# An encoder trunk in fp32: the begin of the MLPs in another order, and the joint to the down projection

## The chip, the cores and the metric

The kernel runs on one core of a Trainium2 chip. The metric is the device time of one execution in microseconds (us), lower is better. The core's engines each take their own list of instructions in order and wait for one another by semaphores: PE multiplies matrices, DVE and ACT work on whole tiles, POOL does tile sums and issues some transfers, SP issues most transfers. TensorE's clock has two levels here, 1.2 and 2.4 GHz; the profile gives the granted clock as a share of the full one.

## The reference

Two requests of 256 and 512 tokens, 768 in all, with 1024 features pass through two layers. Layer 0 has two kinds of attention, layer 1 a differential attention, and each has an MLP behind it:

```
def rmsnorm(x, g, eps=NORM_EPS):
    xf = x.astype(jnp.float32)
    y = xf * lax.rsqrt(jnp.mean(xf * xf, axis=-1, keepdims=True) + eps)
    return (y * g.astype(jnp.float32)).astype(x.dtype)
...
# every layer, after attention: x = x + relu(rmsnorm(x, g) @ w_up) ** 2 @ w_down
```

The hidden width of the MLP is 4096. Everything is fp32.

## The kernel before, in words

**Precision.** Each fp32 operand is halved into a high part (a copy by ACT, L80 for weights, L116 and L119 for activations) and a low part (a subtraction by DVE, L81, L117, L120), and a product is three passes on PE: high by high, high by low, low by high.

**Tokens and features.** Features lie on the partitions, tokens along the rows. The 768 tokens are two halves A and B of 384 (`HT`).

**Up projection** (`product`, L857). It makes the 4096 hidden features in 16 blocks of 256, `mp` 0 to 15. A product is 12 matmuls: four slices of 128, three passes each. The blocks 0 and 1 are made in the plain way, 8 products each, since their operands `c0` to `c3` are the norm-scaled x alone. The blocks 2 to 15 take a scheme with seven products instead of eight: its operands are sums of the four quarters of x (`c4` to `c7`, made once by `second()`, L792 and L117, and kept) and sums of the four quarters of the weights (`weights()`, four sums on POOL, L843, then the halving of four pieces for the products (1,4), (6,5), (7,3) and (2)). The seven results are joined on DVE and ACT into a tile `z` (L865, L926, L939), in which four quarters of 384 tokens lie.

**The norm.** x is multiplied by the norm's gain before the projection, but by the tokens' factor 1/rms only after it. The squares of x are made by ACT and added up on DVE (`acc`, L152), summed over the partitions on PE (`ss`, L161, 12 tiny matmuls), turned into a mean on DVE (`ms`, L164), raised to -1/2 on POOL (`rt`, L166), and spread over all partitions on PE (`pb`, L178) with a copy by DVE (`R`, L180).

**Finishing a block** (`finish`). z is cut at zero and multiplied by R on DVE (L876), squared by ACT (L878), and sent to a buffer `T` in DRAM by ACT's queue (L879); four further quarters `t`, sums of those, are made on DVE (L865, L792) and sent by POOL's queue (L887). For the blocks before R is there, z waits in the list `wait`. Three z tiles exist.

**Down projection** (L1019). It takes the same scheme the other way round: 7 products, each over the whole hidden width in `NG` groups of `ND` = 4 blocks, 28 steps of 48 matmuls. A step's right operand `th` is loaded from T (`operand`, a transfer by SP) and halved by ACT (L116) and DVE (L117); its weights are loaded, summed on POOL (L985) where needed, and halved. The first four steps use four banks of PSUM at once, one each for 256 output features.

**Order.** The program is written in one order for all engines; a scheduler then sets each engine's list by a model of when each instruction could run, so an edit in one place can move instructions elsewhere in the lists. Tiles come from pools with a fixed number of buffers.

## Time and profile before

| | |
|---|---|
| median of 3 runs | 1789.31 us (1788.85 to 1790.62) |
| profiled execution | 1793.21 us |
| its span | 1791.2 us |
| granted clock of TensorE, mean | 0.982 |
| PE busy | 96% of the span |
| DVE busy | 77% |
| ACT busy | 46% |
| POOL busy | 33% |

The profile is of one execution. A row of its timeline begins with the start in us from the span's begin and the busy time in us; then come engine, line of the kernel, operation, the names of what is written and read, and in brackets the idle time before and what ended it. Rows that follow each other closely are put together (x2, x3). A row's time contains its start-up, so consecutive ones overlap a little. PE's matmuls are pipelined, and a few records are missing.

### The profile page before, as it was taken

The numbers are of one execution on the slowest core, as the hardware profiler recorded it, in microseconds if no ns is written. First come the engines' busy times: TensorE is split into PE (matmuls) and PEld (weight loads), VectorE is DVE, ScalarE is ACT, GpSimd is POOL, SyncE is SP. The second block draws the span as 40 slices with busy tenths as digits, with TensorE's granted clock in tenths as the row PEclk, the third lists the DMA queues.
The fourth block names the chain that finished last, engine by engine and source line by source line (L and its number), as shares of the span: only waits on it lengthen the run. The fifth ranks groups of instructions, "written<-read, shape, count | busy, mean of one in ns | idle before, by whom it ended". The sixth has DMA issues, their size and how long they took to land.

```text
span 1791.2 us, 28400 instructions
## 1 busy us (share of the span) xinstructions
PE 1728.0 (96%) x10994; PEld 1644.2 (92%) x10994; DVE 1385.5 (77%) x2182; ACT 827.2 (46%) x1509; POOL 583.7 (33%) x456
## 2 busy tenths in 40 slices
PE   7999999998999999999999999999988999999997
PEld 7887888898999989999999999988988999899997
DVE  7777746597888867799656767776878888787995
ACT  6665544363333444444435555554633334444441
POOL 2321000023555404475021212220225554053750
PEclk8999999999999999999999999999999999999998
DMA  5111223312554587664311101112125545977621
GB/s 173 41 33 37 68 71 104 121 48 72 189 163 164 182 329 294 245 204 158 97 46 48 48 25 45 54 57 95 48 69 180 166 166 170 337 271 258 223 89 71
DMA packets 74598, 235.42 MB, mean 131 GB/s; under 512 B 7904, under 2 KB 25056, under 8 KB 74464
## 3 DMA queue, kind: packets, MB, share of 16 engines
q1 hardware_dynamic: 52480, 186.93, 31.1%
q0 software_dynamic: 7168, 25.17, 3.8%
q10 hardware_dynamic: 14816, 21.52, 3.3%
q8 instruction: 86, 1.41, 0.3%
q14 instruction: 48, 0.39, 0.1%
HBM read 182.47 MB, written 50.33 MB: 130 GB/s over the span
## 4 chain that ended last, share of the span: by engine, by line
PE 79%; DVE 10%; issue 4%; ACT 3%; POOL 2%; DMA 2%; POOLq 0%; DVEq 0%; SPq 0%; ACTq 0%
PE dn L1019 26%; PE up L857 18%; PE dqk L190 8%; PE opa L202 5%; PE dvp L190 4%; PE opb L202 2%; PE npa L202 2%; PE ds L268 2%; PE dpv L716 2%; DVE t L792 2%; DVE wlo L81 1%; PE qp L190 1%; PE vp L190 1%; PE npv L596 1%; PE npb L202 1%
## 5 line engine op out<-in xcount | busy, mean ns | idle before, releaser
L857 PE MATMUL up<-c,whi 128*128 128x384 f32 x1824 | 472.8, 341 | 3.0 <-DVE z L865 3.0
L1019 PE MATMUL dn<-th,whi 128*128 128x384 f32 x1792 | 464.6, 340 | 8.4 <-DVE th L117 5.7
L857 PEld LDWEIGHTS up<-c,whi 128*128 128x128 f32 x1824 | 335.6, 191 | 3.7 <-issue 3.6
L1019 PEld LDWEIGHTS dn<-th,whi 128*128 128x128 f32 x1792 | 328.4, 189 | 9.7 <-DVE th L117 6.3
L857 PE MATMUL up<-c,wlo 128*128 128x384 f32 x912 | 311.0, 342 | 13.3 <-DVE wlo L81 13.1
L1019 PE MATMUL dn<-th,wlo 128*128 128x384 f32 x896 | 304.4, 340 | 0.0
L985 POOL TENSOR_TENSOR ch<-ch,wd 128x1024 f32<-128x1024 f32 x60 | 190.7, 3189 | 127.6 <-DVE wlo L81 97.4
L843 POOL TENSOR_TENSOR s<-wraw 128x512 f32<-128x512 f32 x56 | 91.7, 1652 | 368.8 <-DMA wraw<-in_w_up_dram 284.9
L81 DVE TENSOR_TENSOR wlo<-ch,whi 128x1024 fp32r<-128x1024 f32 x88 | 165.7, 1894 | 36.6 <-ACT whi L80 35.1
L857 PEld LDWEIGHTS up<-c,wlo 128*128 128x128 f32 x912 | 173.9, 191 | 15.4 <-DVE wlo L81 15.4
L80 ACT ACTIVATE whi<-ch 128x1024 fp32r<-128x1024 f32 x88 | 93.4, 1064 | 184.7 <-PE dn L1019 147.1
L1019 PEld LDWEIGHTS dn<-th,wlo 128*128 128x128 f32 x896 | 169.7, 189 | 0.0
L81 DVE TENSOR_TENSOR wlo<-wraw,whi 128x1024 fp32r<-128x1024 f32 (+3 forms) x132 | 146.7, 1114 | 27.5 <-ACT whi L80 27.1
L80 ACT ACTIVATE whi<-wraw 128x1024 fp32r<-128x1024 f32 (+3 forms) x128 | 117.0, 916 | 91.6 <-PE up L857 42.7
L117 DVE TENSOR_TENSOR th<-tr,th 128x1536 fp32r<-128x1536 f32 x56 | 131.3, 2347 | 7.6 <-ACT th L116 7.0
L190 PE MATMUL dqk<-whi,xh 128*128 128x256 f32 x384 | 115.9, 302 | 3.1 <-ACT dv L646 3.1
L190 PE MATMUL dqk<-whi,xl 128*128 128x256 f32 x384 | 108.5, 283 | 0.0
L190 PE MATMUL dqk<-wlo,xh 128*128 128x256 f32 x384 | 108.3, 282 | 0.0
L701 ACT ACTIVATE de<-ds,m 128x512 f32<-128x512 f32 (+1 forms) x96 | 58.3, 612 | 81.7 <-DVE m L699 81.7
L878 ACT ACTIVATE z<-z 128x1536 f32<-128x1536 f32 x32 | 47.7, 1490 | 103.0 <-DVE z L876 103.0
L865 DVE TENSOR_TENSOR z<-up,z 128x384 f32<-128x384 f32 x168 | 92.4, 551 | 2.6 <-issue 1.3
L80 ACT ACTIVATE whi<-s 128x1024 fp32r<-128x1024 f32 x56 | 59.5, 1064 | 67.0 <-PE up L857 67.0
(217 smaller groups left out, 3784.4 us busy)
## 6 DMA issues: line engine op xcount, KB each, us to landing
wd<-in_w_down_dram SPq DMA_DIRECT2D x84, 512.0 KB, 4.1
tr<-T SPq DMA_DIRECT2D x56, 768.0 KB, 5.4
wraw<-in_w_up_dram SPq DMA_DIRECT2D x64, 512.0 KB, 3.6
T<-t POOLq DMA_DIRECT2D x64, 384.0 KB, 3.1
T<-z ACTq DMA_DIRECT2D x32, 576.0 KB, 3.0
ch<-in_w_down_dram SPq DMA_DIRECT2D x28, 512.0 KB, 6.0
wraw<-in_w_in_o_dram SPq DMA_DIRECT2D x24, 512.0 KB, 3.6
wraw<-in_w_in_e_dram SPq DMA_DIRECT2D x16, 512.0 KB, 3.6
```

Of the source, the lines that this page charges most:

```text
L80: nc.scalar.activation(hi, raw, AF.Copy)
L81: nc.vector.tensor_tensor(out=lo, in0=raw, in1=hi.bitcast(F32), op=ALU.subtract)
L117: nc.vector.tensor_tensor(out=lo, in0=src, in1=hi.bitcast(F32), op=ALU.subtract)
L190: nc.tensor.matmul(ps[:, :256], st[:, tk], col(k, part, 0, 256), start=(k == 0 and i == 0), stop=(k == KD - 1 and i == 2))
L202: nc.tensor.matmul(ps[:, : e - s], w, mv[:, s:e], start=(k == 0 and i == 0), stop=(k == nk - 1 and i == 2))
L701: nc.scalar.activation(e, s, AF.Exp, bias=m, scale=1.0, accum_out=l2[:, c : c + 1])
L843: nc.gpsimd.tensor_tensor(out=d_, in0=x_, in1=y_, op=ALU.add)
L857: nc.tensor.matmul(ps, part[a_][:, base + k * P : base + (k + 1) * P], t[:, b_], start=start and k + i == 0, stop=stop and k == 3 and i == 2)
L865: nc.vector.tensor_tensor(out=out, in0=x_, in1=y_, op=op)
L878: nc.scalar.activation(z, z, AF.Square)
L985: nc.gpsimd.tensor_tensor(out=t, in0=t, in1=new.pop((i, rp)), op=ALU.add)
L1019: nc.tensor.matmul(ps, w[a_][:, c : c + P], th[:, b_, q], start=i + q + k == 0, stop=i == NG - 1 and q == ND - 1 and k == 2)
```

## The change

The changes lie in `mlp` (both layers), and in the norm behind layer 0's MLP.

- `weights()`: the four sums on POOL are written ahead of all splits; the splits come in the order (1,4), (7,3), (2), (6,5) instead of (1,4), (6,5), (7,3), (2).
- `finish()`: of the two tiles for sums, the first is taken from another pool in even blocks.
- The norm's squares are written ahead of the plain products; the column sums and `rt` after the first half of the second plain block; the spreading to R right behind the plain blocks, ahead of block 2. Before, squares and column sums stood behind block 2, the spreading behind the first product of block 3.
- The weights of block 2 are written ahead of `second()`.
- The waiting z of blocks 0 and 1 are finished inside block 2, and block 2's own z at its end; before, all three at the begin of block 3.
- In each block the sum with p3 stands ahead of the product p5.
- Down projection, step 0: for all four banks the passes with the high half of `th` come first, then those with the low half.
- Norm behind layer 0's MLP: squares in two tiles in turn.

```
-            for ps_, t in (((1, 4), raws[0]), ((6, 5), sa), ((7, 3), sb), ((2,), raws[1])):
-                if t is sa:
-                    for d_, x_, y_ in ((s1, a21, a22), (s2, s1, a11), (s3, a11, a21), (s4, a12, s2)):
-                        nc.gpsimd.tensor_tensor(out=d_, in0=x_, in1=y_, op=ALU.add)
+            for d_, x_, y_ in ((s1, a21, a22), (s2, s1, a11), (s3, a11, a21), (s4, a12, s2)):
+                nc.gpsimd.tensor_tensor(out=d_, in0=x_, in1=y_, op=ALU.add)
+            for ps_, t in (((1, 4), raws[0]), ((7, 3), sb), ((2,), raws[1]), ((6, 5), sa)):
...
+            if mp == FF // 256 - 1:
+                ta, tb = (up.tile([P, 1024], F32, tag="s", name="t", bufs=3)[:, :NT].rearrange("p (a t) -> p a t", a=2) for _ in range(2))
+            else:
+                ta, tb = (xo_tile("t").rearrange("p (a t) -> p a t", a=2) if mp % 2 == 0 and n == 0 else
+                          g1.tile([P, 2, HT], F32, tag="c0", name="t", bufs=4) for n in range(2))
...
         ws = [weights(True) for _ in range(2)]
+        for k in MO:
+            nm.add(x[k])
         for w in ws:
...
+                if last == 0 and wait:
+                    rt = nm.rstd()
...
             if len(wait) == 1:
+                w2 = weights()
                 second()
+        R.append(nm.spread(rt))
...
-            w = weights()
+            w = weights() if mp > 2 else w2
             one = lambda n: product(bank(n), w[n], n)
             p1 = one(1)
-            if mp == 3:
-                R.append(nm.spread(rt))
-                while wait:
-                    finish(wait.pop(0))
...
             add(z11, p2, z11)
+            if mp == 2:
+                finish(wait.pop(0))
             p4 = one(4)
             add(z22, one(7), z12)
             add(z21, p4, z22, ALU.subtract)
+            add(z12, p3, z12)
+            if mp == 2:
+                finish(wait.pop(0))
             p5 = one(5)
             nc.vector.scalar_tensor_tensor(out=z22, in0=p5, scalar=-1.0, in1=z22, op0=ALU.mult, op1=ALU.subtract)
             add(z12, p5, z12)
-            add(z12, p3, z12)
-            if mp == 2:
-                for k in range(KD):
-                    nm.add(x[k])
-                rt = nm.rstd()
-                wait.append(z)
-            else:
-                finish(z)
+            finish(z)
...
+            for passes in (((0, 0), (1, 0)), ((0, 1),)) if s == 0 else (((0, 0), (0, 1), (1, 0)),):
+                for r, ps in enumerate(banks):
+                    w = parts[n, i, r // 2]
+                    for q in range(ND):
+                        c = (r % 2) * 512 + q * P
+                        for a_, b_ in passes:
+                            nc.tensor.matmul(ps, w[a_][:, c : c + P], th[:, b_, q], start=i + q + a_ + b_ == 0,
+                                             stop=i == NG - 1 and q == ND - 1 and a_ == 1)
...
-        nxt, nn = [None] * KD, Norm(sq)
+        nxt, nn = [None] * KD, Norm(sq2)
```

**PE, begin of layer 0's MLP.** The rows are matmuls in PE's order; `up_` is a product's bank (4951 is the last product of block 2, 5026 the first of block 3, 5082 the second), `c` an operand. Before:

```order
L857 MATMUL up_4951<-c5_4733,whi_4855 128x384 x2
L857 MATMUL up_4951<-c5_4733,wlo_4856 128x384
L161 MATMUL ss_4989<-ones_77,acc_4327 128x2 x6
L857 MATMUL up_5026<-c1_4374,whi_5006 128x384 x2
...
L857 MATMUL up_5026<-c1_4512,wlo_5007 128x384
L178 MATMUL pb_5040<-ident_72,rt_4998 128x128 x4
L178 MATMUL pb_5046<-ident_72,rt_4998 128x128 x2
L857 MATMUL up_5082<-c3_4380,whi_5018 128x384 x2
```

Now (up_4788 and up_4785 belong to the second plain block, up_4911 is the first product of block 2):

```order
L856 MATMUL up_4788<-c3_4518,wlo_4552 128x384
L161 MATMUL ss_4837<-ones_77,acc_4327 128x2 x6
L856 MATMUL up_4785<-c2_4377,whi_4555 128x384 x2
...
L856 MATMUL up_4788<-c0_4521,wlo_4556 128x384
L178 MATMUL pb_4901<-ident_72,rt_4846 128x128 x4
L178 MATMUL pb_4907<-ident_72,rt_4846 128x128 x2
L856 MATMUL up_4911<-c1_4374,whi_4696 128x384 x2
```

The column sums moved from behind block 2 into the second plain block (behind 12 of the 16 plain products), and the spreading from behind block 3's first product to the place between the plain blocks and block 2.

**DVE, the same place.** The rows show the end of the list of operand sums and what follows. `t` and `c4` to `c7` are operand sums, `s` sums of weights, `z` the joined products. Before (s_4846 is the piece for the products 7 and 3 of block 2):

```order
L117 TENSOR_TENSOR c5_4733<-t_4718,c5_4733 128x384
L81 TENSOR_TENSOR wlo_4860<-s_4846,whi_4859 128x1024
L152 TENSOR_TENSOR acc_4327<-acc_4327,sq_4986 128x768
L81 TENSOR_TENSOR wlo_4864<-wraw_4843,whi_4863 128x512
L81 TENSOR_TENSOR wlo_5007<-wraw_5000,whi_5006 128x1024
...
L865 TENSOR_TENSOR z_4880<-up_4951,z_4880 128x384
L164 TENSOR_SCALAR ms_4996<-ss_4989 128x6
...
L180 COPY R_5039<-pb_5040 128x512
```

Now (s_4690 is the piece for the products 6 and 5 of block 2):

```order
L81 TENSOR_TENSOR wlo_4705<-wraw_4688,whi_4704 128x512
...
L792 SCALAR_TENSOR_TENSOR t_4766<-x1_4250,gains_81,t_4766 128x384
L164 TENSOR_SCALAR ms_4844<-ss_4837 128x6
L792 SCALAR_TENSOR_TENSOR t_4766<-x1_4319,gains_81,t_4766 128x384 x3
L117 TENSOR_TENSOR c6_4770<-t_4766,c6_4770 128x384
L117 TENSOR_TENSOR c7_4778<-t_4766,c7_4778 128x384
L117 TENSOR_TENSOR c4_4774<-t_4766,c4_4774 128x384
L117 TENSOR_TENSOR c5_4781<-t_4766,c5_4781 128x384
L81 TENSOR_TENSOR wlo_4709<-s_4690,whi_4708 128x1024
L180 COPY R_4900<-pb_4901 128x512
L180 COPY R_4900<-pb_4907 128x256
```

All acc now stand earlier in the list, the `ms` stands inside it with eight instructions behind, and R is copied straight after the list.

**PE, the joint of layer 0.** dn_6872 to dn_6875 are the four banks, th_6746 the operand of step 0 and th_6852 that of step 1; a matmul with `wlo` takes the high half of th, one of each two with `whi` in the old order the low half. Before:

```order
L1019 MATMUL dn_6872<-th_6746,whi_6842 128x384
L1019 MATMUL dn_6873<-th_6746,whi_6842 128x384
L1019 MATMUL dn_6874<-th_6746,whi_6846 128x384
L1019 MATMUL dn_6875<-th_6746,whi_6846 128x384
L1019 MATMUL dn_6872<-th_6746,whi_6842 128x384
L1019 MATMUL dn_6872<-th_6746,wlo_6843 128x384
L1019 MATMUL dn_6872<-th_6746,whi_6842 128x384 x2
```

Now:

```order
L1022 MATMUL dn_6872<-th_6746,whi_6842 128x384
L1022 MATMUL dn_6872<-th_6746,wlo_6843 128x384
...
L1022 MATMUL dn_6875<-th_6746,wlo_6847 128x384
L1022 MATMUL dn_6872<-th_6746,whi_6842 128x384 x4
L1022 MATMUL dn_6873<-th_6746,whi_6842 128x384 x4
L1022 MATMUL dn_6874<-th_6746,whi_6846 128x384 x4
L1022 MATMUL dn_6875<-th_6746,whi_6846 128x384 x4
L1022 MATMUL dn_6872<-th_6852,whi_6864 128x384 x2
```

Before, the fifth matmul was the first to take the low half of th; now 32 matmuls, high and low weights in turn over the four banks, stand ahead of the 16 that take it.

## Rows read from the trace of the kernel before

**Rows 1.** The page: busy time of an engine with its share of the span, and the groups of the up projection with their counts (busy us, mean ns, idle before).

```profile
PE 1728.0 (96%) x10994; PEld 1644.2 (92%) x10994; DVE 1385.5 (77%) x2182; ACT 827.2 (46%) x1509; POOL 583.7 (33%) x456
...
L857 PE MATMUL up<-c,whi 128*128 128x384 f32 x1824 | 472.8, 341 | 3.0 <-DVE z L865 3.0
...
L857 PE MATMUL up<-c,wlo 128*128 128x384 f32 x912 | 311.0, 342 | 13.3 <-DVE wlo L81 13.1
```

**Rows 2.** What PE waited for: us in total, times, longest us.

```profile
PE up L857 <- DVE wlo L81: 13.1, 5, 3.8
PE pb L178 <- POOL rt L166: 5.8, 3, 2.3
PE dn L1019 <- DVE th L117: 5.7, 2, 2.8
...
PE dqk L190 <- ACT dv L646: 3.1, 1, 3.1
PE up L857 <- DVE z L865: 3.0, 2, 1.8
PE dn L1019 <- DVE z L865: 2.7, 2, 1.4
```

**Rows 3.** Table of stretches, start and end in us from the span's begin: length, busy us (instructions) of PE, PEld, DVE, ACT, POOL, granted clock, share of the DMA engines, GB/s. First row: layer 0 from the first up matmul to the first down one; second: undisturbed blocks; third: the begin of its down projection; fourth and fifth: layer 1's up projection and joint.

```profile
375.79:632.21 256.42, 246.84 (x1395) 245.63 (x1394) 220.62 (x266) 105.34 (x126) 122.42 (x87) 0.98 0.43 148
462.00:627.00 165.00, 165.00 (x946) 165.00 (x945) 145.08 (x170) 66.27 (x68) 92.28 (x65) 1.00 0.51 171
632.21:648.00 15.79, 11.60 (x50) 10.95 (x50) 12.06 (x12) 5.88 (x6) 1.45 (x2) 0.78 0.92 351
1272.20:1531.66 259.46, 248.15 (x1394) 246.04 (x1393) 223.20 (x267) 105.43 (x127) 123.22 (x87) 0.98 0.44 149
...
1531.66:1548.00 16.34, 12.15 (x59) 11.50 (x59) 12.58 (x13) 7.54 (x7) 1.45 (x2) 0.90 0.86 313
```

**Rows 4.** Timeline of PE, begin of layer 0's MLP. Sixteen matmuls lie from 416.00 up to 421.29.

```profile
416.00 0.69 PE L857 MATMUL up<-c,wlo 128*128 128x384 f32 x1 [3.80 <-DVE wlo L81]
...
421.29 0.54 PE L857 MATMUL up<-c,whi 128*128 128x384 f32 x2
...
430.85 1.26 PE L161 MATMUL ss<-ones,acc 128*128 128x2 f32 x10
...
436.60 1.60 PE L178 MATMUL pb<-ident,rt 128*128 128x128 f32 x12 [2.28 <-POOL rt L166]
```

**Rows 5.** Timeline of PE, begin of layer 1's MLP. Ten matmuls lie from 1312.35 up to 1315.68.

```profile
1312.35 0.69 PE L857 MATMUL up<-c,wlo 128*128 128x384 f32 x1 [3.79 <-DVE wlo L81]
...
1315.68 0.50 PE L857 MATMUL up<-c,whi 128*128 128x384 f32 x2
...
1332.01 2.33 PE L178 MATMUL pb<-ident,rt 128*128 128x128 f32 x12 [2.29 <-POOL rt L166]
```

**Rows 6.** Timeline of DVE, the list at the begin of layer 0's MLP, the mean (ms) behind it, and the last instruction of the list of layer 1.

```profile
382.13 3.01 DVE L152 TENSOR_TENSOR acc<-acc,sq 128x768 f32<-128x768 f32 x3
...
386.49 4.02 DVE L152 TENSOR_TENSOR acc<-acc,sq 128x768 f32<-128x768 f32 x2
...
411.26 1.67 DVE L792 SCALAR_TENSOR_TENSOR t<-x,gains,t 128x384 f32<-128x384 f32 x3
412.85 1.96 DVE L117 TENSOR_TENSOR c<-t,c 128x384 fp32r<-128x384 f32 x4
414.72 1.22 DVE L81 TENSOR_TENSOR wlo<-s,whi 128x1024 fp32r<-128x1024 f32 x1
...
416.73 0.69 DVE L81 TENSOR_TENSOR wlo<-wraw,whi 128x512 fp32r<-128x512 f32 x1
...
432.14 0.16 DVE L164 TENSOR_SCALAR ms<-ss 128x6 f32<-128x6 f32 x1
...
1314.08 0.69 DVE L81 TENSOR_TENSOR wlo<-wraw,whi 128x512 fp32r<-128x512 f32 x1
```

**Rows 7.** POOL: the last sum of weights in the list's time, from the timeline, and the durations of all `rt` (ns min/median/max).

```profile
406.05 1.61 POOL L843 TENSOR_TENSOR s<-wraw,s 128x512 f32<-128x512 f32 x1
...
L166 POOL TENSOR_TENSOR rt<-ms,nhalf x6: 848/1424/2267, 25.6 to 1780.7; 128x6 f32<-128x6 f32 x4, 128x3 f32<-128x3 f32 x2
```

**Rows 8.** Timeline of PE, the joint of layer 0. Sixteen matmuls lie from 637.53 up to 642.82.

```profile
637.53 0.69 PE L1019 MATMUL dn<-th,whi 128*128 128x384 f32 x1 [2.84 <-DVE th L117]
...
642.82 0.69 PE L1019 MATMUL dn<-th,whi 128*128 128x384 f32 x2
```

**Rows 9.** Timeline of DVE, the joint of layer 0.

```profile
632.41 0.56 DVE L939 SCALAR_TENSOR_TENSOR z<-up,z 128x384 f32<-128x384 f32 x1 [0.93 <-PE up L857]
632.88 1.14 DVE L865 TENSOR_TENSOR z<-up,z 128x384 f32<-128x384 f32 x2
634.05 1.76 DVE L876 SCALAR_TENSOR_TENSOR z<-z,R 128x1536 f32<-128x1536 f32 x1
635.73 3.42 DVE L117 TENSOR_TENSOR th<-tr,th 128x1536 fp32r<-128x1536 f32 x2
```

**Rows 10.** The joint of layer 0: ACT's timeline at the halving of step 1's operand, POOL's at the issue of the transfer in front of it, and the time of POOL's transfers from issue to landing (min/median/max).

```profile
635.87 1.48 ACT L116 ACTIVATE th<-tr 128x1536 fp32r<-128x1536 f32 x1 [5.29 <-DVE z L876]
...
627.14 0.72 POOL L887 DMA_DIRECT2D T<-t  x1 [0.46 <-DVE t L865]
...
DMA to landing us min/median/max: 2.9/3.1/8.4
```

More of the change, by code (lines that the diff above doesn't have):

```diff
@@ L879, in finish @@
             nc.scalar.dma_start(T[i][:, 0:3, q], z_[:, 1:4])
-            ta, tb = (g1.tile([P, 2, HT], F32, tag="c0", name="t", bufs=4) if mp < FF // 256 - 1 else
-                      up.tile([P, 1024], F32, tag="s", name="t", bufs=3)[:, :NT].rearrange("p (a t) -> p a t", a=2)
-                      for _ in range(2))
+            if mp == FF // 256 - 1:
[3 more added lines that the diff above has]
+                          g1.tile([P, 2, HT], F32, tag="c0", name="t", bufs=4) for n in range(2))
             add(ta, z_[:, 1:3], z_[:, 0:1].broadcast_to([P, 2, HT]), ALU.subtract)
@@ L1013, in mlp @@
             th = ths.pop(0)
-            for r, ps in enumerate(banks):
-                w = parts[n, i, r // 2]
-                for q in range(ND):
-                    c = (r % 2) * 512 + q * P
-                    for k, (a_, b_) in enumerate(((0, 0), (0, 1), (1, 0))):
-                        nc.tensor.matmul(ps, w[a_][:, c : c + P], th[:, b_, q],
-                                         start=i + q + k == 0, stop=i == NG - 1 and q == ND - 1 and k == 2)
+            for passes in (((0, 0), (1, 0)), ((0, 1),)) if s == 0 else (((0, 0), (0, 1), (1, 0)),):
[6 more added lines that the diff above has]
+                                             stop=i == NG - 1 and q == ND - 1 and a_ == 1)
             if i == NG - 1:
```

## The prediction

> **What bounds the kernel now.** The page first: PE is busy for 96% of the span [rows 1], so time can only come from PE's waits and from stretches at the lower clock. The list of what PE waits for comes next [rows 2], then a table of stretches [rows 3] that shows how much more than the products the two places of the change cost, then the timelines of PE, DVE, POOL and ACT there [rows 4 to 10].
>
> The price of one matmul of an MLP, undisturbed, is 165.00 us / 946 = 0.1744 us [rows 3]. A layer's up projection issues 1368 of them (half of 1824 + 912 [rows 1]): 238.6 us. To that belong the norm's column sums (1.26 us) and the spreading of its result (1.60 us) [rows 4]: 241.5 us. The stretches took 256.42 and 259.46 us [rows 3], so 14.9 and 18.0 us are lost, 32.9 in all. At the joint, 15.79 us hold 50 down matmuls (8.7 us) and 16.34 us hold 59 (10.3 us): 7.1 and 6.0 us lost, 13.1 in all. What the change can reach is thus 46 us, the bound from above.
>
> The reader should see two causes. At the begin, DVE works off one list without a gap: squares' additions, operand sums t, their low halves c and the weights' low halves. PE runs through the 16 plain blocks and the first product of the third 256 columns, and stands 3.80 us until the list's last-but-two instruction, the wlo of 414.72, is done; the next 16 matmuls then take 5.29 us instead of 2.79, so 2.5 us more at the clock's lower level [rows 4, 6]. In layer 1 it is 3.79 us, and 10 matmuls in 3.33 instead of 1.74 us, 1.6 more [rows 5]. Then PE stands 2.28 and 2.29 us for rt [rows 4, 5], and since three z are finished together afterwards, again for z and wlo (3.0 us in all for z; 13.1 less 7.6 for wlo) [rows 2]. At the joint the first bank waits for the sum with p3 (2.7 us in two layers) and the second product for the low half th (5.7 us in two layers) [rows 2], after which 16 matmuls take 5.29 us [rows 8].
>
> **The change part by part.**
>
> *The begin.* The set of DVE's instructions in the list is the same but for one: an acc, a wlo and the ms stand earlier, and three t, four c and a wlo are now behind the ms. The list began and ended when its inputs came, so I keep its length: end at 416.73 + 0.69 = 417.4 in layer 0, 1314.8 in layer 1 [rows 6]. What stands behind the ms took, from 411.26 to 415.94, 4.7 us [rows 6]. The ms itself takes 0.16 us [rows 6], so it ends near 412.9 and 1310.2. On POOL rt stands behind the sums for the fourth 256 columns, the last of which ended at 407.7 [rows 7], so it starts at once; its length is 0.85 to 2.27 us, median 1.42 [rows 7], and I take the median: 414.3 and 1311.6. PE reaches the spreading after 192 plain matmuls and the column sums, 33.5 + 1.26 = 34.7 us: at 410.5 and 1306.9. It stands 3.8 and 4.7 us, and it stands in front of all products of the third 256 columns, since PE takes its instructions in order: nothing hides this wait. A stand of 3.8 us was followed by 2.5 and by 1.6 us at the lower clock [rows 4, 5]; I take 2.0 for each. New loss: 8.5 + 4.0 = 12.5 us. Bounds of a stand: 0 if DVE's list is 5 us shorter, 7 us if the rt takes its 2.27 us and the list grows by 2.
>
> What was there before goes: weights split (7,3) come early in the list, so p3 waits for nothing; after the spreading DVE's two finished z stand between product sums, and the low halves for the fourth 256 columns have 14.6 us (84 matmuls) for some 13 us of work (145.08 of 165.00 us are busy in the steady stretch, 12.9 per 14.7 [rows 3]), with two z to finish besides the block's own work instead of three at once. I find no second stand; a z costs 1.76 us for its product with R [rows 9], perhaps half as much again while POOL adds. The gain of the begin lies between two counts: all that is lost, 32.9 - 12.5 = 20.4; or only the stands and the two slow stretches that have rows, 13.1 + 3.0 + 4.6 + 4.1 = 24.8, less 12.5 = 12.3. I take the middle, 16.4, because the new order will have small waits of its own that I cannot name.
>
> *The four sums on POOL ahead of the splits, and the fifth tile for ta* add no instruction. The sums now begin when both loads have landed and fall on other instructions of DVE. The price of such a meeting is seen in the list: two acc take 4.02 us beside POOL's sums, three take 3.01 us without, so 2.0 against 1.0 each [rows 6]. The Trainium skill, GPSIMD Engine Reference, section "Specifications", says that the SBUF interfaces are shared with VectorE, with contention for DVE instructions that have two SBUF inputs; the acc rows agree, and by that rule the price follows POOL's busy time, which the change leaves as it is. I take 0, within -2 and +3 us, covered by the 1.8 us per 256 columns that DVE is idle.
>
> *The joint.* The sum with p3 stands ahead of p5's product, so the first bank is free: 2.7 us gone. The pass with th's low half begins after 32 matmuls, 5.6 us from the joint's begin at T, 632.2. DVE from T + 0.2: the sum with p5 and one more (to T + 1.2), the product with R 1.76, th 1.71 (half of 3.42) [rows 9]: T + 4.7. Slack 0.9 us; 5.7 us gone, and with them the slow stretches. Next is step 1, at T + 8.4: its th is made by ACT once POOL's transfer has landed, issued at 627.14 with up to 8.4 us to landing [rows 10], ready as before near T + 5, and its low weights behind th and a t on DVE, about T + 8.5 to 8.9 against T + 8.8. I charge 0.5 us a layer, 1.0 in all: gain 13.1 - 1.0 = 12.1, within 8 and 13.
>
> *The norm after layer 0* gets its squares in two tiles in turn. PE's wait there, 3.1 us for dv [rows 2], does not depend on it; 0, within 1 either way.
>
> Sum: 16.4 + 12.1 = 28.5 us. The profiled execution took 1793.21 us; 1764.7. It lay 3.9 us above the median of the runs, 1789.31, so the forecast is 1760.8, said as 1761.
>
> **The rivals.**
> (A) The stands for z and wlo in the fourth and fifth 256 columns stay, because DVE, still behind after its list, has two z to finish. For it: DVE is 88% busy even in the steady stretch, so a backlog goes slowly. Against: the old backlog was three z with all of the splits at once. Price: 3.0 + 5.5 plus some 4 at the lower clock, 12.5: 1773.
> (B) No stand at the spreading: POOL's sums, now begun at once, overlap other instructions and the list ends 5 us earlier. Price -8.5 - 4.0: 1748. Against: POOL's sums still lie within the list.
> (C) The joint's gain is given back in steps 1 and 2, whose operands hang on transfers; the DMA engines are 92% busy there [rows 3]. For it: the landing of 8.4 us. Against: step 1's th was ready in time before. Price 4 us a layer: 1769.
> (D) Slower. The spreading in front of 84 products makes PE wait for the whole of DVE's list, and this list grows because POOL's sums, begun earlier, meet more of its t, c and acc, at 2.0 instead of 1.0 us. Every us that the ms is later costs one on PE in each layer; at 14 us (half of 28.5) the gain is gone, and at 20 us it is 1761 + 40 = 1801. Against: POOL is busy for some 14 us in the list and already slows it in that time.
> (E) The change does not do what it says: the stands only move, at the begin to the spreading (10 us a layer) and at the joint to step 1: 1787 to 1791.
>
> **How the numbers follow.** Forecast 0.57, A 0.12, B 0.09, C 0.14, D 0.04, E 0.04. The forecast's own range is 1755 to 1768 (stands 2.5 to 6 us, half of the distance between the two counts of the begin, the joint's bounds). The range of 1750 to 1773 takes C whole and the nearer halves of A and B; outside lie the rest of A and B, D, E, and a small part of the forecast, about 0.2. A measurement of this kernel can tell 0.2%, 3.6 us, from no change. Forecast, A, B, C are faster: 0.92; E is the same for the most part, 0.04; D is slower, 0.04.
>
> **What would show it.** Right: PE's list has the spreading waiting for rt some 4 us in each MLP, right behind the plain blocks and followed by a few slow matmuls; no wait for wlo above 1 us in the first five blocks of 256 columns, none for z, and at the joint none for th or z above 1 us. The stretches from the first up matmul to the first down one take 247 to 252 us. Wrong, by A: waits up<-z or up<-wlo near 440 to 460. By B: no wait at the spreading. By C: dn waits for wlo or th 8 to 17 us after the joint. By D: a wait of over 14 us at the spreading. The forecast falls if the ms comes at another time than 4.7 us ahead of the list's end, or if the low halves of the fourth 256 columns are later than their products.

## The result, and the profile after

The changed kernel takes 1766.14 us (median, 1764.83 to 1770.48), the kernel before 1789.26 us: ratio 0.9874, interval 0.9856 to 0.9891. The change is faster by 23 us; the forecast was 28, and the range held the time. The profiled execution took 1770.48 us, 4.3 us above its median, as that of before lay 3.9 above its own, so stretches of the two profiles can be set side by side.

First what PE waited for, in us, times, longest; these lines answer to [rows 2].

```profile
PE pb L178 <- POOL rt L166: 9.9, 3, 5.0
...
PE up L856 <- DVE wlo L81: 3.6, 10, 0.5
PE dqk L190 <- ACT dv L646: 2.2, 1, 2.2
...
PE dn L1022 <- DVE wlo L81: 0.5, 2, 0.3
```

The five long waits for wlo, those for z and those for th are gone. Two things are new: the spreading (pb) waits longer, and there are ten short waits for wlo, all more than 150 us behind the first up matmul of their layer, where the kernel before had none. Then the table of stretches, as [rows 3]: up projection and joint of each layer, and two pieces of layer 0's middle.

```profile
374.98:627.70 252.72, 246.95 (x1395) 244.05 (x1393) 227.16 (x264) 104.20 (x126) 129.89 (x87) 0.99 0.46 150
427.00:530.00 103.00, 103.00 (x590) 102.77 (x590) 93.05 (x105) 37.89 (x41) 59.89 (x40) 1.00 0.51 167
530.00:620.00 90.00, 87.98 (x495) 85.65 (x494) 80.51 (x90) 33.47 (x36) 51.25 (x35) 1.00 0.50 168
627.70:643.49 15.79, 15.54 (x87) 15.00 (x87) 14.90 (x16) 9.12 (x8) 1.45 (x2) 1.00 1.02 393
1261.15:1514.48 253.33, 246.56 (x1395) 244.16 (x1394) 227.68 (x266) 104.34 (x126) 129.40 (x87) 0.99 0.45 151
1514.48:1530.82 16.34, 16.11 (x91) 15.56 (x91) 15.40 (x17) 9.45 (x8) 1.45 (x2) 1.00 0.99 368
```

At the joint 87 matmuls stand where 50 stood, with the clock at 1.00: that place is clean. The up projections became only 3.7 and 6.1 us shorter. In layer 0 the matmul's price is 0.1746 us from 427 to 530 (103.00 / 590) and 0.1818 from 530 to 620 (90.00 / 495): the loss lies late, far behind the begin.

The begin itself, PE's timeline and then DVE's and POOL's, as [rows 4, 6, 7]:

```profile
414.02 2.93 PE L178 MATMUL pb<-ident,rt 128*128 128x128 f32 x12 [3.76 <-POOL rt L166]
416.60 0.99 PE L856 MATMUL up<-c,whi 128*128 128x384 f32 x2
...
420.18 0.33 PE L856 MATMUL up<-c,wlo 128*128 128x384 f32 x1
...
1301.38 2.93 PE L178 MATMUL pb<-ident,rt 128*128 128x128 f32 x12 [4.96 <-POOL rt L166]
```

```profile
412.04 0.15 DVE L164 TENSOR_SCALAR ms<-ss 128x6 f32<-128x6 f32 x1
412.15 1.68 DVE L792 SCALAR_TENSOR_TENSOR t<-x,gains,t 128x384 f32<-128x384 f32 x3
413.75 1.95 DVE L117 TENSOR_TENSOR c<-t,c 128x384 fp32r<-128x384 f32 x4
415.89 1.23 DVE L81 TENSOR_TENSOR wlo<-s,whi 128x1024 fp32r<-128x1024 f32 x1 [0.19 <-ACT whi L80]
...
412.27 1.69 POOL L166 TENSOR_TENSOR rt<-ms,nhalf 128x6 f32<-128x6 f32 x1 [8.22 <-DVE ms L164]
```

DVE's list runs over the mean without a pause, rt starts at once, and PE, done with the plain blocks, stands until rt is there. The spreading then takes 2.93 us instead of 1.60 (in layer 1 instead of 2.33), and the 11 matmuls from 416.60 to 420.18 take 3.58 us instead of the 1.92 that 11 undisturbed ones take. The table of these two stretches has the granted clock, third number from the end, at 0.50 and 0.52, which is the lower level:

```profile
414.02:416.60 2.58, 2.58 (x12) 2.58 (x13) 2.39 (x5) 2.22 (x5) 0.00 (x0) 0.50 0.00 0
416.60:420.18 3.58, 3.58 (x13) 3.58 (x13) 3.55 (x5) 0.00 (x0) 0.00 (x0) 0.52 0.00 0
```

Where the 23.0 us between the two spans (1791.2 and 1768.2) came from, cut at the first up matmul and the first down matmul of each layer: ahead of layer 0's MLP 0.8; up projection of layer 0 3.7; its down projection and layer 1's attention 6.5; up projection of layer 1 6.2 (its row in [rows 3] begins 0.06 us behind the first matmul, hence 6.1 above); its down projection 5.8.

### The profile page after: what moved, and what is told of

The parts are those of the page before. It is cut to its first block, busy times and chain, and to the rows that moved or that the text cites. A ratio compares the mean times of both kernels' runs of the same rounds, so it can differ in the third digit from the quotient of the medians.

```text
span 1768.2 us, 28354 instructions
## 1 busy us (share of the span) xinstructions
PE 1721.2 (97%) x10994; PEld 1635.5 (92%) x10994; DVE 1396.3 (79%) x2182; ACT 825.0 (47%) x1509; POOL 593.0 (34%) x456
## 4 chain that ended last, share of the span: by engine, by line
PE 67%; DVE 18%; issue 7%; ACT 4%; POOL 2%; DMA 1%; DVEq 0%; POOLq 0%; SPq 0%; ACTq 0%
PE dn L1022 25%; PE dqk L190 8%; PE up L856 6%; PE opa L202 5%; PE dvp L190 4%; DVE z L875 3%; DVE wlo L81 3%; DVE z L864 3%; PE opb L202 3%; PE npa L202 2%; DVE t L864 2%; PE ds L268 2%; PE dpv L716 2%; ACT z L877 2%; DVE t L792 2%
## 5 line engine op out<-in xcount | busy, mean ns | idle before, releaser
L841 POOL TENSOR_TENSOR s<-wraw 128x512 f32<-128x512 f32 x56 | 105.8, 1907 | 331.6 <-DMA wraw<-in_w_up_dram 308.0
L117 DVE TENSOR_TENSOR th<-tr,th 128x1536 fp32r<-128x1536 f32 x56 | 142.8, 2553 | 12.8 <-ACT th L116 12.7
L81 DVE TENSOR_TENSOR wlo<-wraw,whi 128x1024 fp32r<-128x1024 f32 (+3 forms) x132 | 136.3, 1034 | 17.5 <-ACT whi L80 17.0
L116 ACT ACTIVATE th<-tr 128x1536 fp32r<-128x1536 f32 x56 | 82.8, 1478 | 24.4 <-DMA tr<-T 15.6
```

The costliest lines, as they stand in the source:

```text
L81: nc.vector.tensor_tensor(out=lo, in0=raw, in1=hi.bitcast(F32), op=ALU.subtract)
L116: nc.scalar.activation(hi, src, AF.Copy)
L117: nc.vector.tensor_tensor(out=lo, in0=src, in1=hi.bitcast(F32), op=ALU.subtract)
L841: nc.gpsimd.tensor_tensor(out=d_, in0=x_, in1=y_, op=ALU.add)
```

## The experiments

Twelve kernels were run, each beside the kernel before on the same chip. The table has the medians and the two up projections of each profile, cut as above; for the kernel before they are 256.4 and 259.5, for the changed one 252.7 and 253.3.

| run | median, us | ratio to before (interval) | up, layer 0 and 1, us |
|---|---|---|---|
| joint_only | 1785.36 | 0.9985 (0.9977 to 0.9994) | 260.9, 259.9 |
| begin_only | 1772.52 | 0.9913 (0.9899 to 0.9926) | 248.8, 249.3 |
| old_weights | 1769.33 | 0.9896 (0.9883 to 0.9910) | 251.8, 254.1 |
| spread_p2 | 1763.08 | 0.9858 (0.9845 to 0.9872) | 249.1, 249.8 |
| p3_last | 1767.43 | 0.9878 (0.9862 to 0.9895) | 248.7, 249.7 |
| p3_last_spread | 1761.01 | 0.9840 (0.9827 to 0.9854) | 245.5, 246.1 |
| p3_last_oldw | 1759.95 | 0.9840 (0.9827 to 0.9854) | 248.8, 249.0 |
| half_sums | 1751.23 | 0.9789 (0.9776 to 0.9802) | 243.8, 246.6 |
| best_a | 1759.69 | 0.9843 (0.9828 to 0.9858) | 246.4, 248.2 |
| best_b | 1766.82 | 0.9882 (0.9866 to 0.9897) | 251.1, 251.9 |
| passes_old | 1780.91 | 0.9956 (0.9943 to 0.9969) | 252.6, 253.0 |
| best_c | 1756.04 | 0.9820 (0.9806 to 0.9834) | 244.9, 246.5 |

**The parts by themselves.** First the joint's part alone, on the kernel before:

```
             add(z21, p4, z22, ALU.subtract)
+            add(z12, p3, z12)
             p5 = one(5)
...
-            add(z12, p3, z12)
...
+            for passes in (((0, 0), (1, 0)), ((0, 1),)) if s == 0 else (((0, 0), (0, 1), (1, 0)),):
```

> The kernel before with the joint's part of the change alone: step 0 takes the high half of th for all four banks first, and the sum with p3 stands ahead of p5's product. Theory: the joint lost 13 us in the two layers and loses under 1 us now, and the rest of the order has nothing to do with it, so 1789.3 - 12 = 1777 us, with the waits for th and z at the joint gone and the waits for wlo, rt and z at the begin of the MLPs as they were. Rival 1: the earlier sum with p3 also disturbs every block (new waits for wlo in the middle of the up projection), 1781 to 1784. Rival 2: the gain needs the new begin too, 1786 or more.

Only 3 us came. What PE waited for:

```profile
PE up L857 <- DVE wlo L81: 10.6, 9, 3.8
PE pb L178 <- POOL rt L166: 5.9, 3, 2.5
...
PE up L857 <- DVE z L865: 5.2, 4, 2.3
...
PE dn L1020 <- DVE th L117: 1.4, 2, 0.8
...
PE dn L1020 <- DVE wlo L81: 0.3, 1, 0.3
```

The waits at the joint fell from 8.4 us to 1.7, and the two stretches behind the joints became 10.4 us shorter together, but layer 0's up projection grew by 4.5 us (layer 1's by 0.4), and waits for z and wlo came in more places. By the waits rival 1 holds: the sum's new place has a price in the blocks. By its time rival 2 holds as well (0.9985 of 1789.3 us is 1786.6): with the old begin most of the gain is lost again. Then the other half, the changed kernel with both edits of the joint undone:

> The changed kernel with the joint's part undone. Theory: the joint's waits of the kernel before come back, 12 us, so 1766.1 + 12 = 1778 us; the spreading waits 3.8 and 5.0 us for rt as in the changed kernel, and the small waits for wlo in the middle of the up projection (0.2 to 0.5 us each) stay, since they come from POOL's sums being written ahead of the splits. Rival: those waits come from the sum with p3 standing ahead of p5, and go: 1770 us.

1772.5 us is nearer to the rival, 2.5 us above it. The joint's waits are back, with 12.2 us more in the two stretches behind the joints, and the up projections are 4 us a layer shorter than in the changed kernel, with no wait for wlo at all. So my theory of POOL's sums written ahead of the splits as the source of the short waits falls: those stand here as in the changed kernel. The passes were undone too; that it is the sum with p3 and not they is shown below (p3_last). The direct test of the theory, the old weights() in the changed kernel, agrees:

```
-            for d_, x_, y_ in ((s1, a21, a22), (s2, s1, a11), (s3, a11, a21), (s4, a12, s2)):
-                nc.gpsimd.tensor_tensor(out=d_, in0=x_, in1=y_, op=ALU.add)
-            for ps_, t in (((1, 4), raws[0]), ((7, 3), sb), ((2,), raws[1]), ((6, 5), sa)):
+            for ps_, t in (((1, 4), raws[0]), ((6, 5), sa), ((7, 3), sb), ((2,), raws[1])):
+                if t is sa:
...
```

> The changed kernel with weights() as before: the sums on POOL behind the first split, and the order (1,4), (6,5), (7,3), (2). Theory: in the changed kernel a block of the middle of the up projection takes 15.3 us instead of 14.65 because POOL's sums begin as soon as the loads have landed and then lie beside DVE's longest instructions (z times R 2.74 instead of 2.29 us, wlo of the sums 1.41 instead of 1.22); DVE's chain of a block, with its 1.56 us for ACT's square, then is longer than PE's. Undone, the block takes 14.65 again, 8 us come back in the two layers, and the begin costs the same: 1758 us, no wait of PE for wlo in the middle. Rival 1: the split order is what lets p3 start at once in block 2; without it PE stands 2 to 4 us more there in each layer, 1762 to 1766. Rival 2: the longer blocks come from the two finishes inside block 2 (a backlog of DVE) or from the earlier sum with p3: 1766 us, waits as they were.

1769.3 us, no gain: the up projections stay near 252 and 254 us. The waits listed fell, from 3.6 us in ten to 1.4 us in four, but they are no full measure of the loss. Counted from one matmul's start to the next, against the undisturbed 0.1744 us, PE loses 4.1 and 3.5 us in the two layers of the changed kernel from 100 us behind the first up matmul on, and 2.7 and 4.2 us here, most of it outside the waits that the list has.

**The place of the spreading.** It was moved behind three products of block 2:

```
-        R.append(nm.spread(rt))
...
             p3, p2 = one(3), one(2)
+            if mp == 2:
+                R.append(nm.spread(rt))
```

> The changed kernel with the spreading placed behind the products p1, p3 and p2 of block 2 instead of ahead of them. Theory: the stand at the spreading (3.8 and 5.0 us) and what follows it (the spreading and some 12 matmuls at the clock's lower level, 1.3 + 1.7 us a layer) are the price of its place; 36 matmuls, 6.3 us, cover the wait, and nothing else is late, since the low weights of (6,5) are done 4.7 us after the mean. 1766.1 - 14 = 1752 us. Rival: the whole wait moves to p6, whose low weights stand at the end of DVE's list, 2 to 3 us a layer left with its slow stretch: 1758 to 1761 us. Rival 2: R is late for the two finishes in block 2, and waits for z or wlo come back in block 3: 1762 or more.

The stand at the spreading is gone, as expected, but the two up projections are only 7.1 us shorter and the median 3 us, instead of 14. (The spans of the two profiles differ by 7.3 us; that of the changed kernel was taken in an execution 4.3 us above its median, this one 1.1 above.) PE then waits 1.1 and 1.9 us in block 3 for a wlo, and the short waits of the middle begin at 502 us instead of 537: part of what PE gained at the begin it met again later, since DVE was not faster.

**The sum with p3.** Early in the last block alone:

```
             add(z21, p4, z22, ALU.subtract)
-            add(z12, p3, z12)
+            if mp == FF // 256 - 1:
+                add(z12, p3, z12)
...
             add(z12, p5, z12)
+            if mp < FF // 256 - 1:
+                add(z12, p3, z12)
             finish(z)
```

> The changed kernel, but the sum with p3 stands ahead of p5's product in the last block only; in the others it is behind p5 again, as before. The run with the joint undone had no wait for wlo in the middle of the up projection, and its two up projections took 248.8 and 249.3 us instead of 252.7 and 253.3. Theory: it is the place of this one sum in all blocks that makes DVE's chain of a block longer than PE's 14.65 us, and only the last block needs it at the joint. 1766.1 - 8 = 1758 us, no wait for wlo in the middle, and the joint as clean as in the changed kernel. Rival: the middle was clean there for another reason (the old step 0 lets the scheduler order the blocks otherwise): 1766 us with the waits.

The time did not move, and yet the theory's first half holds. The waits:

```profile
PE pb L178 <- POOL rt L166: 9.7, 3, 4.8
...
PE dn L1025 <- ACT th L116: 3.3, 2, 2.0
...
PE dn L1025 <- DVE th L117: 1.7, 2, 1.0
```

None for wlo in the up projection, which is 4.1 and 3.6 us shorter; from 100 us behind its begin on PE loses nothing against 0.1744 us a matmul. The stretches behind the joints gave it back, 4.3 and 4.6 us longer: the first step of the down projection runs clean, and then step 1 waits for its operand, because in this kernel the scheduler put the load of step 1's operand behind four loads of weights on SP (in layer 0 issued 1.0 us behind the joint's begin and landed 8.2 behind it; in the changed kernel issued 10.6 us ahead of it) and its halving behind three halvings of weights on ACT. That neither theory nor rival had in it. The same, with the spreading late:

> As the run before this one, and the spreading placed behind p1, p3 and p2 of block 2. With the spreading alone so placed, PE's stand there went from 9 us to nothing, but only 3 us came back, since the waits for wlo in the middle began two blocks earlier. Theory: in the changed kernel DVE is the bound from the first block on, and PE's gain at the begin is only lent until DVE's backlog reaches it; with DVE's chain short again PE is the bound and the gain stays: 1758 - 12 = 1746 us, with at most 1 to 2 us of waiting left in block 3 of each layer. Rival: the stand is replaced by another that is not DVE's: 1755 us or more.

1761 us, with the same wait at step 1; the late spreading brings 3 us a layer, not 6. With the old weights() instead:

> The changed kernel with the sum with p3 early in the last block only, and with weights() as before. Theory: with DVE's chain short, the place of POOL's sums and the order of the splits is worth little either way: 1756 to 1760 us, no wait for wlo in the middle. Rival 1: the sums ahead of the splits are the cause of the middle waits too, and this is faster than the new weights() by 2 to 4 us: 1754 to 1756. Rival 2: the old split order makes p3 of block 2 wait: 1762 or more.

1760.0 us, the upper end of the theory's range. The up projections are those of the other run within 0.7 us, so with the spreading early the new weights() changes nothing there; here the scheduler kept step 1's operand early, and the joint stayed clean.

Why one sum in another place makes DVE late is seen in the groups of DVE's instructions by shape, from 475 to 620 us: first before, then the changed kernel, then the sum early in the last block only (busy us, mean ns of one).

```profile
L81 DVE TENSOR_TENSOR wlo<-s,whi 128x1024 fp32r<-128x1024 f32 x20 | 24.3, 1216 | 0.0
L876 DVE SCALAR_TENSOR_TENSOR z<-z,R 128x1536 f32<-128x1536 f32 x10 | 22.9, 2290 | 0.3
L865 DVE TENSOR_TENSOR t<-z 128x768 f32<-128x768 f32 x10 | 17.8, 1782 | 15.6 <-ACT z L878 15.6
```

```profile
L81 DVE TENSOR_TENSOR wlo<-s,whi 128x1024 fp32r<-128x1024 f32 x20 | 28.3, 1413 | 0.0
L875 DVE SCALAR_TENSOR_TENSOR z<-z,R 128x1536 f32<-128x1536 f32 x10 | 27.3, 2735 | 0.0
L864 DVE TENSOR_TENSOR t<-z 128x768 f32<-128x768 f32 x9 | 15.9, 1761 | 14.0 <-ACT z L877 14.0
```

```profile
L81 DVE TENSOR_TENSOR wlo<-s,whi 128x1024 fp32r<-128x1024 f32 x19 | 28.8, 1517 | 0.0
L875 DVE SCALAR_TENSOR_TENSOR z<-z,R 128x1536 f32<-128x1536 f32 x10 | 22.2, 2218 | 0.3
L864 DVE TENSOR_TENSOR t<-z 128x768 f32<-128x768 f32 x10 | 13.8, 1378 | 15.6 <-ACT z L877 15.6
```

The instructions are the same, their durations are not: POOL's sums slow now this one and now that one. For z times R, which takes 1.76 us alone, the traces show how. Here is one block's end in the changed kernel, DVE and then POOL's sum at that time, and the same with the sum early in the last block only:

```profile
571.79 1.22 DVE L81 TENSOR_TENSOR wlo<-s,whi 128x1024 fp32r<-128x1024 f32 x1
572.92 2.85 DVE L875 SCALAR_TENSOR_TENSOR z<-z,R 128x1536 f32<-128x1536 f32 x1
...
571.92 2.24 POOL L841 TENSOR_TENSOR s<-wraw 128x512 f32<-128x512 f32 x1 [5.15 <-DMA wraw<-in_w_up_dram]
```

```profile
563.79 1.38 DVE L81 TENSOR_TENSOR wlo<-s,whi 128x1024 fp32r<-128x1024 f32 x1
565.09 0.55 DVE L864 TENSOR_TENSOR z<-up,z 128x384 f32<-128x384 f32 x1
565.67 2.27 DVE L875 SCALAR_TENSOR_TENSOR z<-z,R 128x1536 f32<-128x1536 f32 x1
...
564.05 2.27 POOL L841 TENSOR_TENSOR s<-wraw 128x512 f32<-128x512 f32 x1
```

In both, POOL's sum ends 1.15 us behind the end of the wlo (574.16 against 573.01, 566.32 against 565.17), and z times R ends 1.61 to 1.62 us behind that sum (575.77, 567.94). What differs is what DVE does in between. The z sum of 0.55 us, which reads PSUM, runs at its usual length beside POOL's sum and covers part of the wait; in the changed kernel it has moved away, and z times R stands straight behind the wlo. These two distances return in nearly all middle blocks of the fourteen traces where a sum of POOL runs there, and the length follows the instruction ahead: 2.27 us behind a z sum (the kernel before, begin_only, the three p3_last, best_a, best_b, best_c), 2.85 behind a wlo (the changed kernel, joint_only, old_weights, spread_p2, half_sums, passes_old), each time with a few exceptions. So the sum that the change moved was itself the cover, and its early place costs DVE nearly 0.6 us a block. The wlo and the first t vary too, and were not followed in this way.

To see whether POOL is the cause, half of its sums were left out from block 3 on, so that this kernel computes something else:

> The changed kernel without the third and fourth of POOL's sums of weights in the blocks 3 to 15: the products 7 and 3 take the first pair of weights instead, so the output leaves those sums out. DVE's instructions keep their number and nearly their places. Theory: DVE's chain is long because its products z times R and its wlo lie beside POOL's sums (2.74 us instead of 1.76 alone); with half of them gone z times R falls to 2.3 us or less, the chain is shorter than 14.65 us, and PE's waits in the middle vanish: 1758 us. Rival: the chain is long by the order of DVE's instructions and the wait for ACT's square, whatever POOL does: 1764 to 1766 us, waits as they were.

The short waits are gone, 1751.2 us. That is 7 us more than expected, since POOL's sums also lie in the list at the begin: the spreading's stands fell to 1.7 and 2.9 us. One number of the theory was wrong: z times R stayed at 2.63 us on average, since a wlo still stands ahead of it and one of the two sums left still runs there; what became shorter is the first t (1.04 instead of 1.76 us) and the wlo. DVE's busy time in a stretch of 115 us, and PE's, in the changed kernel, then with the sum in the last block only, then with half of the sums:

```profile
480.00:595.00 115.00, 113.39 (x643) 111.65 (x642) 102.06 (x109) 42.42 (x45) 72.13 (x46) 1.00 0.46 155
```

```profile
480.00:595.00 115.00, 115.00 (x660) 115.00 (x659) 100.63 (x120) 45.34 (x48) 69.79 (x48) 1.00 0.52 170
```

```profile
480.00:595.00 115.00, 115.00 (x660) 115.00 (x660) 96.34 (x118) 45.99 (x48) 44.01 (x30) 1.00 0.46 161
```

In the first, DVE did 109 instructions in 102.06 us, 0.936 us each; in the second 120 in 100.63, 0.839; in the third 118 in 96.34, 0.816. The two that let PE run at its pace have the cheaper instructions. In the third DVE also waits 5.6 us in this stretch for ACT's high halves of the weights, where in the changed kernel it waits for nothing but ACT's square.

**The joint's two edits apart.** The changed kernel with the old passes (and the old tiles for the squares), the early sum kept:

> The changed kernel with the old order of passes in step 0 of the down projection, and the old tiles for the squares behind layer 0's MLP; the early sum with p3 stays. Theory: of the joint's gain of 12 us the passes carry what hung on th, 2.84 us and the slow stretch of 2.5 us in each layer, 9 to 10 us in all, and the sum with p3 only its 1.35 us a layer; the squares' tiles carry nothing: 1775 us, with waits of dn for th of 2.5 to 3 us and none for z. Rival 1: most of the joint's gain is the sum with p3, since DVE is then done a sum earlier: 1770 or less. Rival 2: the squares' tiles matter: a wait of PE behind the down projection of layer 0 that the changed kernel hasn't.

1780.9 us, 6 us more than expected. The two stretches behind the joints are 14.1 us longer than in the changed kernel, all of the joint's gain and 1.8 us more. Its waits at the joint:

```profile
PE dn L1021 <- DVE th L117: 7.5, 2, 3.8
...
PE dqk L190 <- ACT dv L646: 3.1, 1, 3.1
...
PE dn L1021 <- DVE z L864: 1.2, 2, 0.6
```

The early sum took 0.7 us a layer off the wait for z, and the wait for th grew from 2.84 to 3.77 us by as much and more: it is one chain, and the matmul that wants th's low half is the one that sets it. The passes carry the joint; without them the sum carries nothing. The wait for dv is 3.1 us here and 2.2 in the changed kernel; p3_last has the new tiles and 3.1 as well, so the tiles for the squares do not set it.

**Looking for a faster one.** From p3_last_oldw with the late spreading:

> The changed kernel with the sum with p3 early in the last block only, weights() as before, and the spreading behind p1, p3 and p2 of block 2. The run without the last of these took 1760 us; the spreading so placed brought the up projections of the other two pairs from 252.7 and 253.3 to 249.1 and 249.8, and from 248.7 and 249.7 to 245.5 and 246.1. Theory: the same here, 3.5 us a layer, since the joint stays clean: 1753 us. Rival: the joint's order in the scheduler's list falls back to the one with a late th of step 1, as in the run with the new weights(): 1758 us.

1759.7 us, no gain. With the old order of splits p3's high weights are now late in block 2 (PE up waits for whi, 3.6 us in both layers): once the spreading no longer stands ahead of them, the new order of splits is worth that wait, 1.4 and 2.3 us. Behind it PE waits for z in block 3, 1.8 and 1.1 us, as the kernel before did in later blocks; so the wlo of block 3, which the next run was to remove, is not what is late here.

> As the run before this one, with the finishes spread: the z of blocks 0 and 1 are finished in block 2, that of block 2 in the middle of block 3, that of block 3 at its end. With the spreading late, what PE still waits for is a wlo of block 3 (1.3 and 1.9 us, with a slow stretch behind) that stands on DVE behind three finishes. Theory: with two finishes ahead of it this wait goes, 2 to 3 us a layer: 1748 us. Rival: the wait is for weights that are late themselves (POOL's sums of block 3 begin behind the wlo that frees their tile): 1753 us, the wait as it was.

1766.8 us, slower than without. The waits for whi (3.7 us) and z (2.4 us) stay, and waits for wlo are back (3.9 us, nine times), most in block 3 and later blocks; why spreading the finishes makes DVE later was not tried further.

> The changed kernel with the sum with p3 behind p5 in every block as in the kernel before, the spreading behind p1, p3 and p2 of block 2, and the operand of step 1 of the down projection loaded and halved right behind that of step 0, which in the runs with the sum early in the last block only stood behind four loads of weights on SP and three halvings on ACT. Theory: the sum with p3 is needed early nowhere, since with the new passes its bank is the third of step 0 and is first used 16 matmuls, 2.8 us, after the joint's begin; the two up projections take 245.5 and 246.1 us as in the run with the spreading late and the sum early only in the last block, and the joint is clean again, which gives back 7 us of that run's 1761: 1754 us, no wait of dn for z or th. Rival 1: the sum behind p5 costs at the joint what it cost before (1.35 us and a slow stretch a layer), 1758 us. Rival 2: the early load of step 1 runs into the transfers of block 14 and 15 and delays step 0's weights: waits of dn for wlo, 1760.

1756.0 us, 2 us above its theory, the fastest with the full computation, 10 us below the changed kernel. What PE waited for in the MLPs:

```profile
PE up L856 <- DVE wlo L81: 4.0, 3, 2.0
...
PE dn L1022 <- DVE wlo L81: 2.2, 2, 1.1
```

No wait for z or th at the joint though the sum with p3 is behind p5 in all blocks; 1.1 us a layer for the low weights of step 1, which now stand behind its operand.

## Why the prediction was right, and where it was off

*The stand at the spreading* was 3.76 and 4.96 us, forecast 3.8 and 4.7. The step from the list's end back to the mean held: forecast 37.1 us behind the first up matmul, measured 412.19 - 374.98 = 37.2 us in layer 0. What followed it was dearer: 1.3 us for the slower spreading, which I had left out (2.93 us against the 1.60 of the sum), and 1.7 for the slow matmuls, so 14.7 us for both layers instead of 12.5.

*The old waits of the begin* went, as the sum had it. With the sum with p3 out of the way (p3_last) the up projections are 7.8 and 9.8 us shorter than before, 17.6 us; the term was 16.4, and the upper of the two counts that I took the middle of was 20.4.

*The joint* was forecast at 12.1 us. The two stretches that follow the joints became 6.5 and 5.8 us shorter, 12.3, of which 0.9 is the wait for dv, which is 2.2 or 3.1 us in one kernel and another. So the joint itself brought 11.4, and that the sum comes within 0.2 us is in part luck. The attribution was wrong: I gave 2.7 us to the early sum with p3 and the rest to the passes. The early sum brings nothing without the passes (passes_old), and is not needed with them (best_c).

*The step that failed* is the one that priced at nothing what the change does to the blocks in the middle, "I take 0, within -2 and +3 us, covered by the 1.8 us per 256 columns that DVE is idle". It cost 7.7 us (252.7 + 253.3 less 248.7 + 249.7; by the matmuls' starts 4.1 + 3.5), above the bound. The profile of the changed kernel lies 4.3 us above its median, but old_weights, whose profiled execution lies at its median, has the same up projections, 251.8 + 254.1. Two things were wrong in it. The edit that costs is not the one that was meant there, POOL's sums ahead of the splits, but the sum with p3, which I priced at the joint only while it moves in 14 blocks of each layer. And DVE's idle time was no cover. In the kernel before, what DVE waited for from 480 to 595 us:

```profile
DVE t L865 <- ACT z L878: 12.4, 8, 1.6
```

and its busy time in that stretch:

```profile
480.00:595.00 115.00, 115.00 (x660) 115.00 (x659) 102.79 (x120) 44.19 (x47) 67.30 (x47) 1.00 0.50 169
```

102.79 + 12.4 is 115.2 of 115 us: the idle time is DVE's own wait for ACT's square in the middle of its list, once a block, and nothing can slip into it, as DVE takes its instructions in order. DVE had no slack at all, and a few tenths of a us more in each block came out at PE. The rule of the Trainium skill that I weighed (GPSIMD Engine Reference, "Specifications": the SBUF interfaces are shared with VectorE, with contention for DVE instructions with two SBUF inputs) fits these rows: z times R and the wlo of sums have two such inputs and vary from run to run, while z sums, with one input in PSUM, kept 0.55 us, beside POOL's sums too. My reading of it, that the price follows POOL's busy time and so stays, does not hold: with nearly the same number of sums, DVE's z times R took 2.27 or 2.85 us, by how much of POOL's sum was left when it began (0.65 or 1.23 us).

Three things are shown: the sum's place alone brings the short waits (p3_last against the changed kernel), it makes z times R nearly 0.6 us longer in a block (the rows of the block's end above), and the waits go too when half of POOL's sums are left out. That the longer z times R is the whole way from the place to the waits is argued: the wlo and t moved as well, and no run puts another instruction into the gap.

*The signs.* All that were named for "right" came but one: the up projections were to take 247 to 252 us and took 252.7 and 253.3. The range of the time held in spite of the 7.7 us because it was wide enough for them, 12 us on that side.

*The rivals.* A, B, D and E did not come: no wait for z or wlo above 0.5 us is left in the up projections, and at the spreading PE waited what the forecast said. C did not come in the changed kernel either, whose step 1 waits 0.5 us in all for wlo, but it is near: in p3_last step 1 gave back what the middle gained. The offset of 3.9 us from profile to median was 4.3. In sums: of the 28.5 us the begin brought 1.2 more, its dearer spreading included, the middle took 7.7, the joint brought 0.2 more, and the stretch ahead of layer 0's MLP, which the change doesn't touch, was 0.8 shorter: 23.0, the difference of the two spans.

## What to carry to other kernels

Idle time of an engine is cover only if it isn't the engine's own wait in a chain that repeats: add its busy time and its waits for others over a stretch, and if they fill it, every tenth that a neighbour or an order adds there is paid by whoever waits for it. An edit that a change makes for one place (the joint) is to be priced in each place where its line runs, 14 blocks a layer here. Where two engines slow each other, look at what stands between the instructions that meet: here a short sum that isn't slowed was cover for a long product that is, and moving it took the cover away. And where a scheduler sets the lists, undoing one line can move another far away (step 1's operand behind four loads), so a run is to be read by stretches, not by its time alone.

## What the runs showed that was not expected

Behind a stand of PE of 3.8 us or more the 12 small matmuls of the spreading took 2.93 us; behind stands of 1.7 to 2.9 us they took 1.60 to 2.33, and with none 1.50 (spread_p2). The same 1536-column product on DVE took 1.76 us alone, and 2.27 or 2.85 us beside POOL's sums, with the same work on both engines: it ended 1.61 to 1.62 us behind the sum that ran when it began. And of the 14.7 us that the spreading cost, a place where PE doesn't wait for it gave back about half, whether DVE had slack or not: 7.1 us in the up projections where it had none (spread_p2), and 6.8 where it had some (p3_last_spread against p3_last). In the latter the waits of blocks 3 and 4, 4 us in all and slow matmuls behind them, took the rest.
